# A list schedule with new TensorE estimates: cost by form and tiling, changes of tiling counted, matmuls of the present tiling taken first

## The chip, the cores and the metric

The kernel runs on one core of one Trainium2 chip, in one launch. The metric is the time on the device in microseconds (us). The engines have short names in the rows: PE is TensorE, DVE is VectorE, ACT is ScalarE, POOL is GpSimd, SP is SyncE, which issues the DMAs.

## The reference, cut to what matters

Two blocks of two layers each, over 512 tokens of width 1024, all in float32:

```python
for layer in range(2):                       # first block
    x = x + 0.5 * swiglu(rms_norm(x, g), w_gate, w_up, w_down)
    h, mem_n = rms_norm(x, g2), rms_norm(mem, g3)
    mix = mlstm_mixer(h, mem_n, ...) if layer == 0 else dilated_mixer(h, mem_n, k_sh, v_sh, ...)
    x = x + mix
    x = x + 0.5 * swiglu(rms_norm(x, g4), ...)
    if layer == 0: k_sh, v_sh = ...          # shared keys and values, from x
for l in range(2):                           # second block, on x and a context of 256 tokens
    shift, scale, gate = split(silu(c) @ w_mod[l] + b_mod[l])         # and the same from c_ctx
    u = (x * (1 + scale) + shift) @ w_in[l]
    y = concat(rwkv7_both_directions(u), grouped_attention(u), neighbourhood_attention(u)) * silu(gates)
    x = layer_norm(alpha * x + gate * (y @ w_out[l]))
```

The recurrence of the second block (`S = S * decay - (S k) b + v k`, token by token, forward and backward) is what the kernel does in chunks of 32 tokens.

## The kernel before, in words

The kernel is written as if for a NeuronCore, but its calls are only recorded: each becomes an `Op` (line 354) on named tiles, with an estimated time (`_cost`, line 364). `schedule` (line 529) then fixes the order of issue for all engines at once and gives every tile a numbered slot of its kind (`SLOTS`, line 265: 8 PSUM banks `ps`, 4 slots `raw` for weights as loaded, 70 tiles `t` and so on). `emit` (line 552) issues the operations in that order; so every instruction in the profile has the line 568.

`simulate` (line 441) is the list schedule. It is run from the end, which gives each operation a due time (its key), and from the front, where each engine takes, of the operations that are ready, the one with the least key; three such rounds are made. For TensorE there is one exception: operations are either "small" (estimated under 0.1 us, line 362) or not, and one of the present kind is preferred as long as its key is at most `STAY` = 2.0 us behind the best one's (lines 271, 488, 493). `LATENCY` (line 267) is the time from the end of an operation to the start of one that depends on it.

The large products (`proj`, line 698, and `ffn`, line 803) are split in two parts per operand, so three fp32r matmuls of 128x128 weights and up to 512 columns stand for one in float32. All others are float32 matmuls, each of which shows as two records in the trace. Many of them use a part of the array, as their operands have fewer than 128 partitions or fewer than 128 columns of weights. In this text a tiling is such a part, rows by columns, as the rows write it (128\*32: 128 rows, 32 columns). Those that the prediction speaks of:

- 128\*32, `modulation` (line 1358): each of four quarters of the columns of w_mod goes to its own 32 columns of the array (line 1369), 32x512 or 32x256 outputs; `sums` (line 729) does the same with blocks of tokens.
- 128\*64: the outputs of the attentions (`attend`, line 1531), and in the recurrence `pz` (line 1814) and the state's update; two positions, columns 0 and 64.
- 64\*64 and 64\*32: reads of the state S in the chain over the chunks (`rwkv_d`, line 1822).
- In `rwkv_c` (line 1792) the two matmuls of a step have different tilings: `pu` (line 1813, 128\*128) and `pz` (line 1814, 128\*64).

Of the kernel before, what the change touches and what calls it, by code (L numbers as in the profile page):

```python
# [16 lines left out]
P = 128  # L17
# [6 lines left out]
# ------------------------------------------------------------------ host layouts  # L24
# [5 lines left out]
def _wt(w, ksplit=1):  # L30
    """[K, M] -> [M/128, ksplit, 128, K/128/ksplit*128]: one contiguous block per load."""
    k, m = w.shape
    a = w.reshape(ksplit, k // P // ksplit, P, m // P, P).transpose(3, 0, 2, 1, 4)
    return a.reshape(m // P, ksplit, P, -1)


def _wk(w):
    """[K, N] -> [128, K/128*N]: k tiles side by side."""
    k, n = w.shape
    return w.reshape(k // P, P, n).transpose(1, 0, 2).reshape(P, -1)  # L40
# [71 lines left out]
def _rot():  # L112
    """The lhsT of the rope rotation [-x2, x1, -x4, x3] in each half of 64."""
    m = np.zeros((P, P), np.float32)
    for o in (0, 32, 64, 96):
        for j in range(16):
            m[o + 16 + j, o + j] = -1.0
            m[o + j, o + 16 + j] = 1.0
    return m
# [11 lines left out]
def _order(strict):  # L131
    """[128 = (half, beta or eta, i), direction, head parity, chunk of pair, t]: i up to t in the direction's order, in
    the half that holds the chunk; strict: i before t, and eta alone."""
# [28 lines left out]
def _masks():  # L162
    """Selectors of the first block, loaded where they are used."""
# [7 lines left out]
def pack(a):  # L171
    """Lays the inputs out for the chip: permutations, paddings and copies only."""
# [25 lines left out]
    # second block: tiles r3 k3 v3 dd|ad, rg3, aq3, ak, ag3, nq2, nk2, ng2; token-major av|nv  # L198
    q6 = np.arange(384).reshape(6, 64)[[0, 3, 1, 4, 2, 5]].reshape(-1)
    for l in range(2):  # L200
# [9 lines left out]
        # [3 blocks, 8 k tiles, 128, 1024]  # L210
# [22 lines left out]
def _dil_bias(rel):  # L233
    """[4 heads, 128 queries, 512]: previous and own block of group 0, group 1, group 2; entries of rel_bias or NEG."""
# [11 lines left out]
# neighbourhood attention: tokens in the order (column, row); a tile of 128 queries (16 columns) sees 256 keys from here  # L246
# [3 lines left out]
def _na_bias(rpb):  # L250
    """[2 pairs of heads, 4 tiles, 128 queries, 2 x 256 keys]: entries of rpb, or NEG outside the window of columns."""
# [10 lines left out]
# ------------------------------------------------------------------ recording, order and on-chip memory  # L262
# The program is recorded first, as operations on named tiles. A list schedule over estimated times then fixes the
# order in which the operations are issued, and for every tile one of the numbered slots of its kind.
SLOTS = dict(t=70, raw=4, ps=8, big=3, uv=1, S=14, tmp=2, s8=48, s32=16, s64=4)
ENGINES = ("tensor", "vector", "scalar", "gpsimd", "sync")
LATENCY = dict(tensor=0.2, vector=0.14, scalar=0.15, gpsimd=0.15, sync=3.0)
# [24 lines left out]
class Ref:  # L292
    """A recorded tile, or a view of it. v: numbers of the cells it covers, a cell being a column of 32 partitions."""
# [43 lines left out]
class Recorder:  # L337
    """Stands for the NeuronCore: notes (engine, method, arguments) in the current list."""
# [15 lines left out]
class Op:  # L354
    def __init__(self, eng, method, a, k):
# [4 lines left out]
        self.reads = [x for w, x in refs if not w]  # L360
        self.cost = self._cost()
        self.small = self.cost < 0.1 and eng == "tensor"

    def _cost(self):
        """Estimated microseconds on the engine."""
        n = max([x.cols() for x in self.writes + self.reads] or [1])
        ps = any(x.base.kind == "ps" for x in self.reads)
        if self.eng == "tensor":
            n = self.writes[0].cols()
            if self.method == "transpose":  # L370
                return 0.84e-3 * n
            l = self.k["lhsT"]
            f = 1 / 2.4 if l.base.dt == F32R else 4 / 2.4
            half = 0.58 if 16 < l.cols() <= 64 else 1.0
            return 0.002 + 1e-3 * max(n, 64) * f * half
# [15 lines left out]
def weave(parts):  # L391
    """One order for independent lists of operations, each spread evenly by cost."""
# [9 lines left out]
def dependences(ops):  # L402
    """For each operation the earlier ones that it has to follow."""
    writer, readers, last_pe = {}, {}, {}     # per tile: the last writer of each cell; reads since: (operation, cells)
# [36 lines left out]
def simulate(ops, before, after, key, lag, ahead):  # L441
    """A list schedule: of the operations that are ready and whose tiles have slots, each engine takes the one of least
    key. Only the one of least key overall may take the last slots. lag(i, j): time from the end of i to the start of j."""
# [6 lines left out]
    empty = {k: [(0.0, i) for i in range(m)] for k, m in SLOTS.items()}     # (time, slot) of free slots  # L450
    ready, free = [0.0] * n, dict.fromkeys(ENGINES, 0.0)
    wait = {e: [] for e in ENGINES}       # (time, operation): inputs complete at a later time
    can = {e: [] for e in ENGINES}        # (key, operation)
    small = False
# [5 lines left out]
    def room(i, tight):  # L460
        """When the slots that operation i needs are free; None if there are none."""
# [11 lines left out]
    def best(tight):  # L473
        out = None
        for e in ENGINES:
# [4 lines left out]
            for src, time in ((can[e], lambda x: free[e]), (wait[e], lambda x: x[0])):  # L480
                pick = None
                for x in sorted(src):
# [5 lines left out]
                    if pick and ops[i].small != small:  # L488
                        continue
                    at = room(i, tight)  # L490
                    if at is not None:
                        pick = (max(at, time(x)), key[i], i, e, src, x)
                        if e != "tensor" or src is not can[e] or ops[i].small == small:
# [7 lines left out]
    while len(order) < n:  # L501
# [6 lines left out]
        if e == "tensor":  # L508
            small = ops[i].small
# [19 lines left out]
def schedule(ops):  # L529
    """The order of issue, and a slot per tile: a schedule made from the end gives the latest start of each operation;  # L530
    one from the front takes the operations by that. Each further round makes the schedule from the end by the last one
    from the front."""
# [8 lines left out]
    lag = lambda i, j: 0.0 if ops[i].eng == ops[j].eng == "tensor" else LATENCY[ops[i].eng]  # L541
# [10 lines left out]
def emit(tc, ops):  # L552
    """Issues the recorded operations through Tile."""
# [17 lines left out]
# ------------------------------------------------------------------ the program  # L571
class Prog:
# [13 lines left out]
    # ---- memory  # L586
# [9 lines left out]
    def t2(self, shape=(P, T), dt=F32):  # L596
        """A tile of up to 2 KB a partition; two small ones from the same place in the program share a slot."""
# [28 lines left out]
    # ---- order  # L626
    def par(self, *parts):
        """Independent parts of the program, woven together."""
# [9 lines left out]
    # ---- small helpers  # L638
# [29 lines left out]
    def tr(self, out, a):  # L668
        """PE transpose of 128 partitions, exact."""
        self.nc.tensor.transpose(out, a, self.idn)  # L670

    def split(self, h, l, src, scale=None):
        """src (times a per-partition scale) as the exact sum of two 12-bit parts."""
# [7 lines left out]
    def loadw(self, src, n, w):  # L681
        """n columns of weights as parts, a pair per w columns."""
# [15 lines left out]
    def proj(self, src, xh, xl, n=T, cut=None):  # L698
        """One feature-major tile: out[m, t] = sum_d w[d, m] x[d, t]; cut: ranges of tokens, one after the other."""
# [7 lines left out]
    def proj_tm(self, src, ncol, xh, xl, sels):  # L707
        """Token-major: out[t, n] = sum_d x[d, t] w[d, n]; src [128, 8*ncol], k tiles side by side."""
# [8 lines left out]
    def pow(self, out, a):  # L717
        """out = a ** -0.5."""
# [4 lines left out]
    def rsqrt(self, out, src, n, scale, eps):  # L723
        """out = (src * scale + eps) ** -0.5 for n columns."""
# [4 lines left out]
    def sums(self, tiles, nt):  # L729
        """PSUM [128 = i, t, 2 j + h] = sum over half h of the partitions of tiles[j][:, (t, i)]; the tokens' blocks are  # L730
        summed side by side on the tensor engine."""
# [7 lines left out]
    def turn(self, ps, nt):  # L739
        """PSUM [32 nt, 128] transposed, [128, nt, 32]."""  # L740
# [6 lines left out]
    def parts(self, n=T, cnt=KD):  # L747
        """cnt pairs of [128, n] tiles for the parts of a split."""
# [7 lines left out]
    def norm(self, src, gain, n=T):  # L756
        """The parts of gain*x, and the sum over feature tiles of x**2 / 1024."""
# [1320 lines left out]
```

## Time and profile before

| what | value |
|---|---|
| time, median of 3 runs | 3384.07 us (3383.62 to 3389.64) |
| profiled execution, span | 3384.7 us |
| TensorE busy | 3282.6 us, 97% of the span, 21302 matmul records |
| VectorE, ScalarE, GpSimd busy | 65%, 48%, 7% of the span |
| mean granted TensorE clock | 0.987 of full speed |

The profiled execution's only time is its span, from the first instruction to the last; it stands 0.6 us above the median of the runs. In a timeline row, the start of one row less the start of the one before is the time that the earlier row took of the engine; the second number of a row is longer, since it runs to the end of the last matmul, which the next ones overlap. A float32 matmul counts as x2 there, an fp32r matmul as x1.

### The profile page before, as it was taken

What the parts mean: (1) busy time and instruction counts of PE and PEld (TensorE: products, weight loads), DVE (VectorE), ACT (ScalarE), POOL (GpSimd) and SP (SyncE); (2) the same over time, 40 slices, a digit from 0 to 9 for tenths busy, and PEclk for the clock granted to TensorE, in tenths of its full rate; (3) what the DMA queues carried; (4) which work ended last, traced back from release to release, by engine and by line L of the source; (5) the groups of instructions that cost most, each with busy time, mean ns of one, the idle gap of its engine ahead of it and who ended that gap; (6) DMA issues with size and microseconds to landing.
All of it is one profiled execution on the core that took longest, in us unless ns stands there. A gap on an engine that the chain in (4) does not pass through costs nothing.

```text
span 3384.7 us, 55344 instructions
## 1 busy us (share of the span) xinstructions
PE 3282.6 (97%) x21302; PEld 2604.3 (77%) x21302; DVE 2188.4 (65%) x4605; ACT 1611.1 (48%) x3577; POOL 241.4 (7%) x233
## 2 busy tenths in 40 slices
PE   8999999999999999999999999999999898999898
PEld 4688878878877788767887788777777677877677
DVE  5455578475578676444567846677575787585876
ACT  3333455363434345322345735343553873654773
POOL 0000000000000101000001000000121011010101
PEclk9999999999999999999999999999999999999999
DMA  6434433123222333444332332223322233322231
GB/s 212 152 122 130 138 102 107 53 81 108 93 68 88 110 127 117 138 137 132 95 105 74 116 95 89 72 89 107 111 72 81 73 113 101 109 85 87 60 119 47
DMA packets 153489, 348.41 MB, mean 103 GB/s; under 512 B 16645, under 2 KB 60421, under 8 KB 153225
## 3 DMA queue, kind: packets, MB, share of 16 engines
q1 hardware_dynamic: 153224, 344.87, 32.0%
q8 instruction: 167, 2.74, 0.3%
q14 instruction: 98, 0.79, 0.1%
HBM read 315.05 MB, written 29.76 MB: 102 GB/s over the span
## 4 chain that ended last, share of the span: by engine, by line
PE 84%; DVE 7%; ACT 5%; issue 1%; DMA 1%; POOL 1%; SPq 0%; ACTq 0%; POOLq 0%; DVEq 0%
PE ps L568 84%; DVE t L568 5%; ACT t L568 4%; ACT big L568 1%; DVE big L568 1%; DVE s L568 1%; DVE tmp L568 1%; POOL s L568 1%; DMA raw<-in_wgu_dram 1%; ACT uv L568 0%; DMA raw<-in_aw_dram 0%; DMA raw<-in_win_dram 0%; DMA raw<-in_wmod_dram 0%; DVE uv L568 0%; SPq L568 0%
## 5 line engine op out<-in xcount | busy, mean ns | idle before, releaser
L568 PE MATMUL ps<-t,t 128*128 128x512 f32 (+6 forms) x15204 | 2880.3, 352 | 48.2 <-ACT t L568 26.3
L568 PEld LDWEIGHTS ps<-t,t 128*128 128x128 f32 (+2 forms) x15204 | 2282.3, 182 | 549.9 <-issue 93.1
L568 ACT ACTIVATE t<-raw 128x512 fp32r<-128x512 f32 (+1 forms) x962 | 565.0, 612 | 777.3 <-PE ps L568 526.1
L568 DVE TENSOR_TENSOR t<-raw,t 128x512 fp32r<-128x512 f32 (+2 forms) x962 | 626.2, 671 | 295.8 <-PE ps L568 197.4
L568 ACT ACTIVATE t<-t 128x512 f32<-128x512 f32 (+8 forms) x739 | 376.8, 525 | 448.1 <-DVE t L568 251.6
L568 DVE TENSOR_TENSOR t<-t,t 128x256 f32<-128x256 f32 (+7 forms) x812 | 417.8, 544 | 110.7 <-ACT t L568 62.5
L568 DVE TENSOR_TENSOR t<-ps,t 128x512 f32<-128x512 f32 (+3 forms) x274 | 178.9, 658 | 236.7 <-PE ps L568 229.3
L568 ACT ACTIVATE t<-ps 128x512 f32<-128x512 f32 (+9 forms) x446 | 215.0, 513 | 233.2 <-PE ps L568 230.6
L568 POOL TENSOR_TENSOR s<-s,const 128x4 f32<-128x4 f32 (+6 forms) x65 | 99.3, 1530 | 1788.9 <-DVE s L568 1780.6
L568 DVE SCALAR_TENSOR_TENSOR t<-ps,t 128x512 f32<-128x512 f32 (+3 forms) x229 | 148.1, 649 | 106.1 <-PE ps L568 105.2
L568 PE MATMUL ps<-const,t 128*128 128x128 f32 (+1 forms) x1116 | 188.0, 289 | 20.3 <-ACT t L568 11.8
L568 PEld LDWEIGHTS ps<-const,t 128*128 128x128 f32 x1116 | 134.7, 147 | 64.8 <-ACT t L568 27.9
L568 PE MATMUL ps<-uv,t 64*64 64x64 f32 (+1 forms) x2208 | 143.9, 229 | 3.4 <-DVE t L568 1.6
L568 PEld LDWEIGHTS ps<-uv,t 64*64 64x64 f32 (+1 forms) x2208 | 103.3, 135 | 53.0 <-issue 14.4
L568 ACT ACTIVATE t<-t,const 128x256 f32<-128x256 f32 (+3 forms) x165 | 102.0, 645 | 68.8 <-DVE t L568 37.2
L568 ACT ACTIVATE uv<-ps 32x128 f32<-32x128 f32 (+1 forms) x288 | 92.2, 321 | 59.4 <-PE ps L568 55.3
L568 DVE SCALAR_TENSOR_TENSOR t<-t,t 128x512 f32<-128x512 f32 (+2 forms) x116 | 76.6, 662 | 57.6 <-ACT t L568 56.3
L568 DVE TENSOR_TENSOR uv<-uv,ps 32x192 f32<-32x192 f32 x192 | 66.6, 347 | 66.3 <-PE ps L568 58.7
L568 POOL TENSOR_TENSOR S<-S,s 128x192 f32<-128x192 f32 x96 | 62.4, 650 | 601.0 <-DVE S L568 451.7
L568 PE MATMUL ps<-S,t 64*32 64x64 f32 x2112 | 104.1, 224 | 1.0 <-DVE S L568 1.0
L568 ACT ACTIVATE t<-ps,s,s 128x256 f32<-128x256 f32 (+1 forms) x140 | 88.2, 652 | 32.8 <-DVE s L568 32.7
L568 ACT ACTIVATE t<-ps,const 128x256 f32<-128x256 f32 (+1 forms) x100 | 57.1, 576 | 75.6 <-PE ps L568 74.9
(81 smaller groups left out, 1390.4 us busy)
## 6 DMA issues: line engine op xcount, KB each, us to landing
raw<-in_wgu_dram SPq DMA_DIRECT2D x176, 512.0 KB, 3.8
raw<-in_win_dram SPq DMA_DIRECT2D x88, 512.0 KB, 3.7
raw<-in_wd_dram SPq DMA_DIRECT2D x128, 256.0 KB, 2.7
raw<-in_wmod_dram SPq DMA_DIRECT2D x48, 512.0 KB, 3.8
t<-dram SPq DMA_DIRECT2D x68, 256.0 KB, 3.0
dram<-t SPq DMA_DIRECT2D x68, 256.0 KB, 2.0
t<-dram SPq DMA_DIRECT2D x97, 128.0 KB, 2.3
raw<-in_wd_dram SPq DMA_DIRECT2D x64, 192.0 KB, 2.4
```

Source lines behind the costliest of these rows:

```text
L568: getattr(getattr(tc.nc, op.eng), op.method)(*map(real, op.a), **{q: real(v) for q, v in op.k.items()})
```

## The change

The planner's numbers for TensorE are new, and its preference for "the present kind" now goes by the tiling and no longer by the size. Every comment and docstring is also gone, which moves the line of issue from 568 to 583. No operation is added or taken away: both kernels issue the same 17224 matmuls, 4607 VectorE, 3303 ScalarE and 238 GpSimd instructions and 1043 on SyncE's queue; their order and the slots of their tiles differ.

```diff
-LATENCY = dict(tensor=0.2, vector=0.14, scalar=0.15, gpsimd=0.15, sync=3.0)
+LATENCY = dict(tensor=0.22, vector=0.13, scalar=0.15, gpsimd=0.15, sync=3.0)
+INTO_PE = 0.12
+
+SIDE_BY_SIDE = {(128, 128): 1, (128, 64): 2, (128, 32): 4, (64, 128): 2, (64, 64): 4, (64, 32): 6, (32, 128): 4,
+                (32, 64): 6, (32, 32): 8}
+RETILE = 0.12
...
-        self.small = self.cost < 0.1 and eng == "tensor"
+
+    def _tiling(self):
+
+        l = self.reads[0] if self.method == "transpose" else self.k["lhsT"]
+        up = lambda n: 32 if n <= 32 else 64 if n <= 64 else 128
+        return up(32 * l.v.shape[0]), up(l.cols())
...
             if self.method == "transpose":
-                return 0.84e-3 * n
-            l = self.k["lhsT"]
-            f = 1 / 2.4 if l.base.dt == F32R else 4 / 2.4
-            half = 0.58 if 16 < l.cols() <= 64 else 1.0
-            return 0.002 + 1e-3 * max(n, 64) * f * half
+                return 0.003 + 0.833e-3 * n
+            if self.k["lhsT"].base.dt == F32R:
+                return 0.0137 + n / 2400
+            one = max(0.003 + n / 1200, 0.11 if self.tiling[1] == P else 0.08)
+            return 2 * max(one / SIDE_BY_SIDE[self.tiling], 0.02)
...
-                    if pick and ops[i].small != small:
+                    same = ops[i].tiling == tiling
+                    if pick and not same:
                         continue
...
-                        if e != "tensor" or src is not can[e] or ops[i].small == small:
+                        if e != "tensor" or src is not can[e] or same:
                             break
...
-        if e == "tensor":
-            small = ops[i].small
+        if e == "tensor" and ops[i].tiling != tiling:
+            at, tiling = at + RETILE, ops[i].tiling
...
-    lag = lambda i, j: 0.0 if ops[i].eng == ops[j].eng == "tensor" else LATENCY[ops[i].eng]
+    def lag(i, j):
+        pe = ops[j].eng == "tensor"
+        return 0.0 if pe and ops[i].eng == "tensor" else LATENCY[ops[i].eng] + INTO_PE * pe
+
```

What it does to the order of TensorE is shown at three places. In these rows ps, t, raw, uv and const are tiles with their running numbers, which differ between the kernels, and the last word is the size of the output; a row with x4 is four equal instructions.

The first is the start of the program: raw is w_mod of the modulation, and the 128x512 rows are the first product of the feed-forward. Before:

```order
L568 MATMUL ps_185<-raw_149,const_92 32x512
L568 MATMUL ps_183<-t_133,t_178 128x512
L568 MATMUL ps_185<-raw_149,const_92 32x512
L568 MATMUL ps_183<-t_139,t_170 128x512
L568 MATMUL ps_183<-t_133,t_170 128x512
L568 MATMUL ps_183<-t_141,t_178 128x512
L568 MATMUL ps_183<-t_145,t_170 128x512
L568 MATMUL ps_185<-raw_161,const_92 32x512 x2
L568 MATMUL ps_183<-t_141,t_170 128x512
```

After the change:

```order
L583 MATMUL ps_179<-raw_143,const_92 32x512 x2
L583 MATMUL ps_179<-raw_170,const_92 32x512 x2
L583 MATMUL ps_199<-t_133,t_193 128x512
L583 MATMUL ps_199<-t_139,t_187 128x512
L583 MATMUL ps_199<-t_133,t_187 128x512
L583 MATMUL ps_199<-t_145,t_193 128x512
L583 MATMUL ps_199<-t_150,t_187 128x512
```

The modulation's matmuls come two at a time, and the first four are ahead of the feed-forward.

The second is some 200 rows further: the modulation's last block of columns (raw, 32x256 outputs), again beside the feed-forward. Before:

```order
L568 MATMUL ps_709<-raw_643,const_92 32x256
L568 MATMUL ps_696<-t_444,t_646 128x512
L568 MATMUL ps_696<-t_538,t_652 128x512
L568 MATMUL ps_696<-t_543,t_646 128x512
L568 MATMUL ps_709<-raw_643,const_92 32x256
L568 MATMUL ps_696<-t_538,t_646 128x512
L568 MATMUL ps_696<-t_617,t_652 128x512
L568 MATMUL ps_696<-t_623,t_646 128x512
L568 MATMUL ps_709<-raw_643,const_92 32x256
L568 MATMUL ps_696<-t_617,t_646 128x512
L568 MATMUL ps_709<-raw_643,const_92 32x256
```

After the change:

```order
L583 MATMUL ps_179<-raw_590,const_92 32x512 x2
L583 MATMUL ps_684<-raw_616,const_92 32x256 x4
L583 MATMUL ps_672<-t_443,t_605 128x512
L583 MATMUL ps_672<-t_436,t_605 128x512
L583 MATMUL ps_697<-const_230,t_688 128x128 x4
```

The four quarters of one w_mod tile stood apart, one to three other matmuls between them, and now follow each other.

The third is in the recurrence's `rwkv_c` of the second layer: the 64x128 rows are `pz` (128\*64), the 128x64 rows `pu` (128\*128). Before:

```order
L568 MATMUL ps_29557<-t_27846,t_29478 128x512
L568 MATMUL ps_29587<-t_29573,t_29141 64x128
L568 MATMUL ps_29589<-t_29575,t_29573 128x64 x2
L568 MATMUL ps_29587<-t_29573,t_29141 64x128
L568 MATMUL ps_29589<-t_29575,t_29573 128x64
L568 MATMUL ps_29587<-t_29573,t_29141 64x128
L568 MATMUL ps_29589<-t_29575,t_29573 128x64
L568 MATMUL ps_29587<-t_29573,t_29141 64x128
L568 MATMUL ps_29557<-t_27864,t_29591 128x512
```

After the change:

```order
L583 MATMUL ps_29600<-uv_27791,t_29122 64x64 x2
L583 MATMUL ps_29603<-t_29591,t_28917 64x128 x4
L583 MATMUL ps_29608<-t_29594,t_29591 128x64 x4
L583 MATMUL ps_29573<-t_27840,t_29610 128x512
L583 MATMUL ps_29573<-t_27891,t_29373 128x512
```

The two kinds took turns, one by one, and now come four and four.

Over the whole order of TensorE, the number of times that an instruction has another tiling than the one before it goes from 1523 to 1246. The table counts stretches (instructions of one tiling in succession) and rounds (as many of them as have positions of their own in the array, so that a second instruction at a position begins a new round):

| tiling, output columns | stretches before, after | rounds before, after |
|---|---|---|
| 128\*128, all | 560, 447 | not counted |
| 128\*32, 512 | 44, 18 | 44, 21 |
| 128\*32, 256 | 41, 13 | 42, 18 |
| 128\*32, 128 | 37, 33 | 46, 48 |
| 128\*64, 128 | 180, 119 | 445, 428 |
| 128\*64, 64 and 193 | 209, 191 | 409, 401 |
| 64\*128 and 32\*128 | 52, 42 | 80, 76 |
| 64\*64 | 136, 128 | 494, 493 |
| 64\*32 | 265, 256 | 472, 464 |

## Rows read from the trace of the kernel before

**Rows 1.** The page: the span and section 1, busy us of each engine.

```profile
span 3384.7 us, 55344 instructions
...
PE 3282.6 (97%) x21302; PEld 2604.3 (77%) x21302; DVE 2188.4 (65%) x4605; ACT 1611.1 (48%) x3577; POOL 241.4 (7%) x233
```

**Rows 2.** The page's section 4, the chain that ended last, by engine.

```profile
PE 84%; DVE 7%; ACT 5%; issue 1%; DMA 1%; POOL 1%; SPq 0%; ACTq 0%; POOLq 0%; DVEq 0%
```

**Rows 3.** Windows: stretch, length, busy us of engines, granted clock, DMA share, GB/s.

```profile
0.00:250.00 250.00, 238.98 (x1057) 166.46 (x1058) 123.68 (x224) 91.64 (x173) 7.74 (x12) 1.00 0.49 163
...
2650.00:2900.00 250.00, 227.14 (x2385) 190.43 (x2384) 199.64 (x507) 167.75 (x411) 29.71 (x31) 0.95 0.31 96
...
3150.00:3385.00 235.00, 206.24 (x2239) 167.35 (x2237) 175.10 (x454) 139.17 (x347) 23.37 (x26) 0.94 0.24 76
```

**Rows 4.** Waits of PE: for whom, us in total, times, the longest.

```profile
PE ps L568 <- ACT t L568: 40.4, 46, 4.0
...
PE ps L568 <- DMA raw<-in_wmod_dram: 11.0, 1, 11.0
...
PE ps L568 <- DVE uv L568: 1.5, 4, 0.5
PE ps L568 <- DVE S L568: 1.0, 2, 0.7
```

**Rows 5.** Timeline of PE near 1565 us: start, length, tiling, form, records.

```profile
1565.44 0.64 PE L568 MATMUL ps<-raw,const 128*32 128x256 f32 x8
1566.01 1.20 PE L568 MATMUL ps<-t,t 128*128 128x512 f32 x4
1567.13 0.62 PE L568 MATMUL ps<-raw,const 128*32 128x256 f32 x2
1567.68 0.73 PE L568 MATMUL ps<-t,t 128*128 128x512 f32 x2
1568.35 0.62 PE L568 MATMUL ps<-raw,const 128*32 128x256 f32 x2
1568.90 1.88 PE L568 MATMUL ps<-t,t 128*128 128x512 f32 x7
1570.71 0.62 PE L568 MATMUL ps<-raw,const 128*32 128x256 f32 x2
```

**Rows 6.** Timeline of PE, 31 to 39 us.

```profile
31.17 1.07 PE L568 MATMUL ps<-raw,const 128*32 128x512 f32 x8
32.17 5.75 PE L568 MATMUL ps<-t,t 128*128 128x512 f32 x24
37.85 1.04 PE L568 MATMUL ps<-raw,const 128*32 128x512 f32 x2
38.82 0.73 PE L568 MATMUL ps<-t,t 128*128 128x512 f32 x2
```

**Rows 7.** Timeline of PE, 2719 to 2721 us.

```profile
2718.92 1.09 PE L568 MATMUL ps<-t,t 128*64 128x128 f32 x14
2719.93 0.66 PE L568 MATMUL ps<-const,t 128*128 128x128 f32 x4
2720.52 0.43 PE L568 MATMUL ps<-t,t 128*64 128x128 f32 x2
2720.89 0.66 PE L568 MATMUL ps<-const,t 128*128 128x128 f32 x4
```

**Rows 8.** Groups by form, PE: records, busy us and mean ns, idle before.

```profile
L568 PE MATMUL ps<-t,t 128*64 128x128 f32 x1448 | 142.0, 286 | 2.3 <-ACT t L568 1.4 <-ACT uv L568 0.3 <-DVE t L568 0.2
...
L568 PE MATMUL ps<-raw,const 128*32 128x512 f32 x128 | 48.9, 619 | 11.0 <-DMA raw<-in_wmod_dram 11.0
L568 PE MATMUL ps<-t,t 128*128 128x64 f32 x288 | 44.8, 276 | 0.4 <-ACT uv L568 0.3
...
L568 PE MATMUL ps<-raw,const 128*32 128x256 f32 x128 | 25.5, 391 | 0.0
```

**Rows 9.** A window at the start, columns as in Rows 3.

```profile
10.00:15.00 5.00, 3.98 (x5) 0.65 (x5) 4.24 (x8) 3.77 (x8) 0.00 (x0) 1.00 1.04 400
```

More of the change, by code (lines that the diff above doesn't have):

```diff
@@ L360, in __init__ @@
         self.reads = [x for w, x in refs if not w]
+        self.tiling = self._tiling() if eng == "tensor" else None
         self.cost = self._cost()
-        self.small = self.cost < 0.1 and eng == "tensor"
+    def _tiling(self):
+        l = self.reads[0] if self.method == "transpose" else self.k["lhsT"]
+        up = lambda n: 32 if n <= 32 else 64 if n <= 64 else 128
+        return up(32 * l.v.shape[0]), up(l.cols())
     def _cost(self):
@@ L453, in simulate @@
     can = {e: [] for e in ENGINES}
-    small = False
+    tiling = None
     first, head, done, order = sorted(range(n), key=key.__getitem__), 0, [False] * n, []
```

## The prediction

> **What bounds the kernel now.** I read the page's section 1 first: TensorE is busy for 3282.6 of 3384.7 us [rows 1], so all its idle time together is 102.1 us. The chain that ended last says the same from the other side: 84% of it is TensorE's own work, VectorE and ScalarE together have 12% [rows 2]. Then the windows: in the first 250 us TensorE works 239.0 us, and nearly all of what is missing is the first load (11.0 us, one wait [rows 4]); only near the end does it wait much, 22.9 us from 2650 to 2900 and 28.8 us from 3150 to 3385 [rows 3]. So a change that only reorders has two places to act: the 102 us of waiting, and whatever part of the 3283 us of "busy" is not work but the way from one matmul to the next. The second is read from the timeline, where the start of a row less the start of the row before is what that row cost.
>
> **What a change of tiling costs, and what a matmul alone in its tiling costs.** Around 1565 us TensorE alternates between 128\*128 products and the modulation's 128\*32 matmuls [rows 5]. Seven fp32r matmuls take 1570.71 - 1568.90 = 1.81 us, two take 1568.35 - 1567.68 = 0.67; so one more costs 0.228 us, and each such stretch has 0.21 us on top for being entered and left. A 128\*32 stretch costs 0.55 us with one matmul of 256 columns (1567.13 to 1567.68) and 0.57 with four (1565.44 to 1566.01): the four quarters of the array run side by side, and one alone wastes the other three. With 512 columns one takes 0.97 us (37.85 to 38.82) and four 1.00 (31.17 to 32.17) [rows 6]. From 0.55 and 0.97 a round of 512 columns is some 0.84 us, one of 256 some 0.42, and the fixed part of a stretch 0.13. For 128\*64 one matmul of 128 columns takes 0.37 us (2720.52 to 2720.89) and seven, in four rounds of two positions, 1.01 (2718.92 to 2719.93) [rows 7]: 0.213 us a round and 0.157 fixed.
>
> **The sum.** No instruction is added or removed, so every term is a count from the order (the table of stretches and rounds) times one of these prices.
>
> - 128\*128 stretches: 560 to 447. At 0.21 us the 113 are worth 23.7. The price is read from fp32r matmuls; 80 of the 113 begin with one, which gives 16.8. I take 20.
> - 128\*32: with 512 columns 26 stretches at 0.13 and 23 rounds at 0.84, 22.7 us; with 256 columns 28 at 0.13 and 24 at 0.42, 13.7 us; with 128 columns nothing (4 stretches fewer, 2 rounds more). Together 36. That is over half of these forms' busy time, 48.9 and 25.5 us [rows 8], and the second place of the order shows why it can be: one w_mod tile made four stretches of one and now makes one of four.
> - 128\*64: with 128 columns 61 stretches at 0.157 and 17 rounds at 0.213, 13.2 us; the other widths 18 at 0.157 and 8 rounds at about half, 3.7 us. Together 17. Part of it is `rwkv_c`, the third place, whose `pu` matmuls show the same thing: 144 of them (288 records) are busy 44.8 us [rows 8], 0.31 us each, while they alternate with `pz`.
> - The other tilings lose 27 stretches; at 0.157 that is 4 us, an estimate, as no row here prices them.
>
> Sum 77 us of 3282.6. All of it is TensorE's own time and so on the path, except where something else ends last.
>
> Two things come back. At the start the third TensorE instruction now waits for the second w_mod tile, and the feed-forward's first product is queued behind it; on SyncE's queue that tile stands two DMAs of 0.5 MB behind the first. At the 400 GB/s that the window from 10 to 15 us shows [rows 9], 1 MB is 2.6 us; before, work began at 11.0 us with the first tile. Between 0 and 4 us; I take 2. And in the last quarter of TensorE's order, where it waits for ScalarE and VectorE anyway, about 70 of the 277 changes go (809 to 741), a quarter of the sum, 19 us. There a shorter TensorE waits longer for the same chain; I let 8 of the 19 go back, between 0 (all of it lies in the filled parts) and 19.
>
> The new latencies and costs (fp32r 512 columns 0.227 us where the old estimate was 0.215; the row says 0.228) also move ready times on all engines. What that does to the 102 us of waiting the trace of before cannot show. Bounds: waits on ScalarE's and VectorE's tiles may fall by half of the 40.4 us that the largest group has [rows 4], or grow by as much as the present waits near the end, some 25 us in a window [rows 3]. I take nothing.
>
> 3384.7 - 77 + 2 + 8 = 3317.7 us on the profiled execution's span. That execution is 0.6 us above the median of the runs, so 3317 for the median.
>
> A page speaks for a smaller price. The Trainium skill, "TensorEngine Tiling (Array Packing)", section Key Properties, says that a change of tiling mode, not of the tile alone, drains TensorE; "TensorE: Matmul & The Clock Gate", section Step-by-step, puts a drain at about 128 cycles, which at 2.4 GHz would be 53 ns by estimate. Then 277 changes would be worth 15 us. The rows show more per change: 0.21 us for the two ends of an fp32r stretch and 0.13 to 0.16 for those of a narrow one, so a way there and back costs some 0.35 us, not 0.11; and the matmul that runs alone is not in that rule at all.
>
> **The rivals.**
>
> - *The planner's better times also shorten the waits.* For: half of the waiting is on ScalarE's and VectorE's tiles [rows 4], which the added 0.12 us into TensorE would let the planner see coming. Against: TensorE's new speed gives the others less time. 32 us less waiting gives 3285.
> - *Part of the gain becomes waiting.* A stretch of four is issued only when all four have their inputs; raw has four slots, and a w_mod tile that waits for its partner keeps a slot from the weights. For: ScalarE and VectorE are busy 67% and 80% from 2650 to 2900 [rows 3]. Against: in the first 250 us, where most of the modulation's gain lies, TensorE waits only for the first load, and DMA is half idle (0.49). Half of the 77 us gone: 3346.
> - *Only the changes count, not the rounds.* If four quarters in succession still ran one after the other here, because each waits for its load, 277 changes at 0.15 us are 42, less the 10 that come back: 3353. Against: the 0.57 us for four [rows 5].
> - *A change costs what a drain costs*, 53 ns, and nothing else: 3370. The rows speak against it, as shown.
> - *Slower: the preference holds back the recurrence.* A matmul of the chain over the chunks may now stand behind up to 2.0 us of work of the present tiling; before, all large matmuls were one kind. The chain enters TensorE twice a chunk, 16 chunks in two layers and 8 in two contexts, 96 times: at most 192 us. It decides from 77 us, 40% of that, and at half it gives 3317 + 96 = 3413. For: the waits of the last 735 us. Against: TensorE waits only 1.5 and 1.0 us for the chain's own tiles uv and S [rows 4], so the chain has slack, and keys still come first beyond 2 us.
>
> **How the numbers follow.** Forecast 50% (its own range 3298 to 3335: the sum between 65 and 85, the returns between 0 and 20). Shorter waits 14%, half returned 20%, changes alone 7%, drain alone 3%, slower 6%. What a measurement of this kernel can tell from no change is 0.2%, 6.8 us. All cases but the last are beyond that on the fast side, with a little of each lost to "same": faster 0.91, same 0.04, slower 0.05. The range 3282 to 3352 takes in the shorter waits and most of the half returned; left out are changes alone, drain, slower and the tails, under 2 in 10.
>
> **What would show it.** If the sum is right, TensorE's busy time falls to about 3210 us and the idle time stays near 110; the modulation's groups fall from 48.9 and 25.5 us to about 25 and 12, the 128\*64 group of 128 columns from 142.0 to about 130, the 128\*128 group of 64 columns from 44.8 to under 36; the stages before 2450 us shorten by some 55 us, those after by little. If the drain rule holds, the modulation's groups stay. If the recurrence is held back, waits on uv and S grow from 2.5 us to tens, in the last third. It would be wrong in kind if TensorE's busy time fell as said and the span did not.

## The result and the profile after

The changed kernel takes 3326.6 us (median of 4 runs, 3323.7 to 3333.6); the kernel before, beside it, 3385.3 us (3383.6 to 3389.6). The ratio is 0.9826, with a 95% interval of 0.9812 to 0.9840. The forecast was 3317, its range 3282 to 3352.

The page of the changed kernel: the span, section 1 (busy us of each engine) and section 4 (the chain that ended last).

```profile
span 3324.6 us, 55306 instructions
...
PE 3211.6 (97%) x21302; PEld 2597.8 (78%) x21302; DVE 2196.5 (66%) x4605; ACT 1612.8 (49%) x3577; POOL 259.9 (8%) x233
...
PE 79%; DVE 10%; ACT 5%; issue 3%; DMA 1%; POOL 1%; SPq 0%; ACTq 0%; POOLq 0%; DVEq 0%
```

Against [rows 1] TensorE is busy 71.0 us less, and idle 113.0 us instead of 102.1; so the span is 60.1 us shorter. The other engines' busy time is the same within some 20 us. In [rows 2] TensorE's own part of the chain was 84%, now 79%.

Where along the program it went is read from windows (length, busy us of the engines, granted clock). The kernel before, and then the changed one, each up to about its 13,000th matmul record and from there to the end:

```profile
0.00:2450.00 2450.00, 2414.38 (x12984) 1908.58 (x12985) 1525.39 (x3036) 1068.06 (x2301) 121.49 (x113) 1.00 0.34 109
2450.00:3384.70 934.70, 868.21 (x8319) 695.71 (x8318) 662.98 (x1569) 543.06 (x1277) 119.94 (x120) 0.96 0.27 86
```

```profile
0.00:2390.00 2390.00, 2353.09 (x12996) 1906.73 (x12997) 1524.45 (x3039) 1070.45 (x2306) 137.28 (x113) 0.99 0.34 112
2390.00:3324.60 934.60, 858.46 (x8307) 691.09 (x8305) 672.02 (x1566) 542.37 (x1272) 122.66 (x120) 0.96 0.27 86
```

The same number of records is done 60 us sooner, so the whole gain lies in the first part, which has all of the modulation. None remains from the last part, in which seven tenths of the recurrence's matmuls on uv and S run: there TensorE is busy 9.7 us less and idle as much longer. (The order differs, so it is the same number of records and not record for record the same ones.)

The groups by form of the changed kernel (records, busy us, mean ns of one, idle before), for those of [rows 8] and three others:

```profile
L583 PE MATMUL ps<-t,t 128*128 128x512 f32 x9120 | 2260.5, 396 | 11.6 <-DVE t L583 8.4 <-ACT t L583 2.8
...
L583 PE MATMUL ps<-t,t 128*64 128x128 f32 x1448 | 128.0, 285 | 1.9 <-DVE t L583 0.9 <-ACT uv L583 0.6 <-ACT t L583 0.2
L583 PE MATMUL ps<-S,t 64*32 64x64 f32 x2112 | 103.3, 227 | 1.8 <-DVE S L583 1.6
...
L583 PE MATMUL ps<-uv,t 128*64 128x64 f32 x1056 | 92.0, 238 | 6.3 <-DVE t L583 3.4 <-DVE uv L583 1.8 <-ACT t L583 1.0
...
L583 PE MATMUL ps<-t,t 128*128 128x64 f32 x288 | 40.4, 272 | 1.6 <-ACT uv L583 1.3 <-DVE t L583 0.2
...
L583 PE MATMUL ps<-raw,const 128*32 128x512 f32 x128 | 26.3, 632 | 10.7 <-DVE t L583 10.1 <-DMA raw<-in_wmod_dram 0.5
...
L583 PE MATMUL ps<-raw,const 128*32 128x256 f32 x128 | 10.2, 389 | 0.0
```

The modulation's two groups fall by 22.6 and 15.3 us. The mean of one record is unchanged (632 and 389 ns, were 619 and 391): each matmul takes as long as before, but four of them now share that time. The timeline shows it where [rows 5] had rows of x2 (start, length, tiling, form, records):

```profile
1451.51 0.64 PE L583 MATMUL ps<-raw,const 128*32 128x256 f32 x8
1452.08 7.78 PE L583 MATMUL ps<-t,t 128*128 128x512 f32 x33
```

The stretch is a foursome (x8 records) and costs 0.57 us, as the one foursome of [rows 5] did.

### The profile page after: what moved, and what is told of

The parts are those of the page before. It is cut to its first block, busy times and chain, and to the rows that moved or that the text cites. A ratio compares the mean times of both kernels' runs of the same rounds, so it can differ in the third digit from the quotient of the medians.

```text
span 3324.6 us, 55306 instructions
## 1 busy us (share of the span) xinstructions
PE 3211.6 (97%) x21302; PEld 2597.8 (78%) x21302; DVE 2196.5 (66%) x4605; ACT 1612.8 (49%) x3577; POOL 259.9 (8%) x233
## 4 chain that ended last, share of the span: by engine, by line
PE 79%; DVE 10%; ACT 5%; issue 3%; DMA 1%; POOL 1%; SPq 0%; ACTq 0%; POOLq 0%; DVEq 0%
PE ps L583 79%; DVE t L583 7%; ACT t L583 3%; DVE big L583 1%; POOL s L583 1%; DVE s L583 1%; DVE tmp L583 1%; ACT uv L583 1%; ACT big L583 1%; DMA raw<-in_wgu_dram 1%; DVE uv L583 0%; DMA raw<-in_wd_dram 0%; DMA raw<-in_wmod_dram 0%; DMA raw<-in_wkv_dram 0%; DMA dram<-t 0%
## 5 line engine op out<-in xcount | busy, mean ns | idle before, releaser
L583 PE MATMUL ps<-t,t 128*128 128x512 f32 (+6 forms) x15204 | 2839.3, 351 | 44.6 <-DVE t L583 23.4
L583 POOL TENSOR_TENSOR s<-s,const 128x2 f32<-128x2 f32 (+6 forms) x65 | 111.0, 1709 | 1762.8 <-DVE s L583 1762.7
L583 PE MATMUL ps<-const,t 128*128 128x128 f32 x1116 | 188.7, 291 | 30.8 <-DVE t L583 17.4
L583 ACT ACTIVATE t<-t,const 128x256 f32<-128x256 f32 (+3 forms) x165 | 101.9, 646 | 45.0 <-DVE t L583 25.8
L583 ACT ACTIVATE t<-ps,s,s 128x256 f32<-128x256 f32 (+1 forms) x140 | 87.8, 641 | 30.3 <-DVE s L583 25.9
L583 PEld LDWEIGHTS ps<-S,t 64*32 64x32 f32 x2112 | 61.1, 107 | 43.4 <-issue 15.4
```

The costliest lines, as they stand in the source:

```text
L583: getattr(getattr(tc.nc, op.eng), op.method)(*map(real, op.a), **{q: real(v) for q, v in op.k.items()})
```

## The experiments

The theory: TensorE's order by tiling is the whole gain, and its size is the number of stretches and rounds saved times the prices of the prediction. The rivals: the better numbers (costs, latencies) bring it; only the number of changes counts; the price is that of a drain. A question came with the first results: what does the granted clock take back?

For that, the span of each profiled run is split in three. *Idle* is the span less TensorE's busy time. *Clock* is what the stretches at half clock cost: in a run the granted clock is 1.00 or 0.50 of full speed, and an alternation of two small forms that took 0.49 us at full clock took 0.76 at half (shown below), so I count 1 - 0.49/0.76 = 0.355 of the time that TensorE is busy at 0.50. This is an estimate, and a low one, since wider matmuls lose more (below). *Work* is the rest, TensorE's time as if at full clock. *Priced* is the change in work that the counts of the order and the prediction's prices give (0.18 us, 20/113, for a 128\*128 stretch). Each ratio is to runs of the kernel before that were taken beside it (medians 3385.3 to 3387.8 us). The split is of one profiled execution, while the executions of one kernel lie up to 20 us apart, so a few us in it decide nothing.

| kernel | time | ratio to before, 95% | idle | clock | work, change | priced |
|---|---|---|---|---|---|---|
| before | 3385.3 | 1 | 102.1 | 20.4 | 0 | 0 |
| after | 3326.6 | 0.9812 to 0.9840 | 113.0 | 29.0 | -79.6 | -78.4 |
| e1_tiling_only | 3323.4 | 0.9803 to 0.9832 | 101.9 | 31.0 | -74.5 | -78.9 |
| e2_numbers_only | 3422.6 | 1.0088 to 1.0138 | 109.3 | 48.6 | -3.4 | -11.9 |
| e9_latencies_only | 3427.3 | 1.0099 to 1.0129 | 108.5 | 37.6 | +13.8 | +11.9 |
| e10_costs_only | 3407.0 | 1.0043 to 1.0073 | 98.0 | 46.7 | +2.3 | -0.9 |
| e3_all_but_narrow | 3340.9 | 0.9852 to 0.9885 | 106.7 | 25.6 | -59.6 | -59.5 |
| e8_stay1 | 3360.7 | 0.9901 to 0.9946 | 118.6 | 39.8 | -57.9 | -54.5 |
| e5_stay4 | 3327.1 | 0.9805 to 0.9835 | 118.6 | 42.7 | -97.7 | -99.9 |
| e6_no_retile | 3333.2 | 0.9829 to 0.9858 | 118.4 | 42.3 | -87.8 | -93.7 |
| e12_reads_first | 3298.0 | 0.9720 to 0.9751 | 122.1 | 28.8 | -123.7 | -114.7 |
| e14_reads_e1 | 3289.7 | 0.9701 to 0.9733 | 107.6 | 24.2 | -111.7 | -106.2 |
| e16_reads_e1_stay3 | 3300.8 | 0.9719 to 0.9765 | 123.8 | 38.7 | -122.4 | -118.1 |
| e18_reads_e1_f32r | 3289.4 | 0.9692 to 0.9724 | 109.8 | 28.4 | -108.9 | -109.5 |

Over all these orders, the work follows the priced counts within 9 us. How much of that hangs on the 0.355 is seen from fp32r matmuls of 512 columns in a stretch at half clock of the changed kernel (the second row is the matmul behind the six):

```profile
905.55 2.77 PE L583 MATMUL ps<-t,t 128*128 128x512 f32 x6
908.11 0.63 PE L583 MATMUL ps<-t,t 128*128 128x512 f32 x1
```

Each takes 0.427 us where [rows 5] has 0.228, a loss of 0.47. With 0.47 throughout, the changed kernel's work is -82.4 and its clock 11.4 us more than before (8.6 in the table), and work and priced counts lie up to 12 us apart.

**The preference alone, and the numbers alone.** The first is the kernel before with nothing new but the kind that is preferred:

```diff
-        self.small = self.cost < 0.1 and eng == "tensor"
+        self.small = self._tiling() if eng == "tensor" else None
```

> The kernel before, with one edit: the preference goes by the tiling and no longer by the size; all estimated times and latencies stay old. In TensorE's order the stretches of 128*128 fall from 560 to 440, the modulation's 512-column ones from 44 to 24 (rounds 44 to 25), the 256-column ones from 41 to 17 (42 to 20), changes of tiling from 1523 to 1244. Theory (the order by tiling is the gain): TensorE's busy time falls by some 72 us to about 3211, as in the changed kernel, idle time 100 to 125, time about 3328 (3315 to 3345). Rival (the new costs and latencies are the gain): within 10 us of the kernel before, 3375 to 3385.

The second has all the new numbers and the old kinds, and no cost for a change of tiling:

```diff
-                    same = ops[i].tiling == tiling
+                    same = ops[i].small == small
...
-        if e == "tensor" and ops[i].tiling != tiling:
-            at, tiling = at + RETILE, ops[i].tiling
+        if e == "tensor":
+            small = ops[i].small
```

> The changed kernel's costs and latencies, with the old preference by size and no price for a change of tiling. Stretches of 128*128 561 (before 560), modulation 512 columns 34 (44), 256 columns 34 (41), changes 1502 (1523): by the prices of the prediction 12 us less of TensorE. Theory (the order by tiling is the gain): busy time about 3271, time about 3374 (3360 to 3390). Rival (the numbers are the gain, above all by shorter waits): idle time well under 100 us, time 3330 or less.

The preference alone gives 3323.4 us; its interval and that of the whole change overlap. The numbers alone are slower than before by 0.9 to 1.4%, at neither the 3374 of the theory nor the 3330 of the rival. So the gain is the order by tiling, and the numbers, beside it, are worth nothing that can be measured. Where the numbers alone lose is read from the page of that kernel and its windows:

```profile
span 3416.6 us, 55323 instructions
...
PE 3307.4 (97%) x21302; PEld 2633.8 (77%) x21302; DVE 2190.1 (64%) x4605; ACT 1611.7 (47%) x3577; POOL 263.4 (8%) x233
```

```profile
3254.00:3274.60 20.60, 17.18 (x153) 13.57 (x151) 13.65 (x29) 13.91 (x39) 0.00 (x0) 1.00 0.38 112
3274.60:3301.90 27.30, 26.90 (x216) 18.77 (x212) 10.33 (x27) 13.62 (x37) 2.41 (x4) 0.50 0.07 21
3301.90:3325.00 23.10, 23.10 (x307) 17.82 (x306) 15.80 (x48) 13.36 (x42) 2.54 (x5) 1.00 0.39 109
```

Of 166.0 us at half clock (before: 85.4) 27.3 are one stretch. Behind 3.4 us of waiting in 20.6 the clock falls, TensorE then does 216 records in 27.3 us, and when the clock is back 307 in 23.1. Of the 31.9 us that this run is longer, 28.2 are the clock, 7.2 more idle time, and -3.4 work.

**The two kinds of numbers apart**, on the old preference: new latencies only (`LATENCY`, `INTO_PE` and `lag` of the diff), and new costs only (the kernel above with the old `LATENCY` and `INTO_PE` 0).

> The kernel before with the new latencies alone (0.22 and 0.13 instead of 0.2 and 0.14, and 0.12 into TensorE); old costs, old preference. By the prices 12 us more of TensorE's work (128*128 stretches 587 instead of 560, changes 1591 instead of 1523). If the latencies are what made the numbers alone slow (more waiting and more time at the lower clock): 3410 or above, with over 140 us at the lower clock. If they are harmless: 3387 + 12, about 3399, lower clock as before, some 85 to 105 us.

> The new costs alone: old latencies, old preference, no price for a change. By the prices 1 us less than before (574 stretches, 1569 changes, 33 and 34 modulation stretches). If the costs are what made the numbers alone slow: 3410 or above, with over 140 us at the lower clock. If they are harmless: about 3386. If neither of the two is slow, the slowness of both together is an accident of one order.

Both are slower than before, 1.1% and 0.6%. With the latencies the work itself grows by 13.8 us, close to the 11.9 that the counts give: the order has more stretches; the clock takes 17.2 us more. With the costs the work is nearly unchanged (+2.3) and the clock takes 26.3 us more. Both have over 140 us at the lower clock (144.2 and 162.4). Neither shortens the waits by anything like the 32 us of the first rival (idle +6.4 and -4.1 us).

**All but the modulation's tiling.** 128\*32 counts as 128\*128, both for the preference and for the cost of a change:

```diff
+        self.kind = (P, P) if self.tiling == (P, 32) else self.tiling
...
-                    same = ops[i].tiling == tiling
+                    same = ops[i].kind == tiling
```

> The changed kernel, but for the preference and the price of a change the 128*32 tiling counts as 128*128, so these matmuls are again taken as they come. Changes of tiling stay low, 1260 (changed kernel 1246), but the modulation has 34 stretches and 34 rounds of 512 columns (changed kernel 18 and 21) and 34 and 35 of 256 (13 and 18). Theory (a round that runs alone wastes the other positions): 19 us of TensorE more than the changed kernel, the two modulation groups at about 38 and 21 us busy (26.3 and 10.2 in the changed kernel), time about 3344. Rival (only the number of changes of tiling counts): 14 changes at 0.15 us, so no more than 3 us above the changed kernel, 3329.

The order has 1260 changes of tiling, the whole change 1246; yet 3340.9 us against 3326.6, with intervals that do not touch. The modulation's groups of this kernel and a piece of its timeline:

```profile
L585 PE MATMUL ps<-raw,const 128*32 128x512 f32 x128 | 40.6, 633 | 11.3 <-DMA raw<-in_wmod_dram 11.3
...
L585 PE MATMUL ps<-raw,const 128*32 128x256 f32 x128 | 21.8, 391 | 0.0
```

```profile
1471.09 0.96 PE L585 MATMUL ps<-t,t 128*128 128x512 f32 x3
1471.98 0.62 PE L585 MATMUL ps<-raw,const 128*32 128x256 f32 x2
1472.53 0.50 PE L585 MATMUL ps<-t,t 128*128 128x512 f32 x1
```

They keep 14.3 and 11.6 us that the whole change takes out; over all groups the work is 20.0 us more, 19 were expected. A single matmul here has its stretch of 0.55 us to itself again. The number of changes alone is not the measure; how many matmuls run side by side within one stretch counts too. The Trainium skill's rule from "TensorEngine Tiling (Array Packing)", Key Properties, that a change of mode drains TensorE, has no term for this; the row, 0.55 us for one and 0.57 for four, decides.

**How long the preference may hold out**, and without the cost of a change: `STAY` 1.0 and 4.0 instead of 2.0, `RETILE` 0.0 instead of 0.12.

> The changed kernel with STAY 1.0 instead of 2.0. Changes 1333 (1246), 128*128 stretches 486 (447), modulation rounds 28 and 20 (21 and 18): 24 us more of TensorE's work by the prices. Theory: about 3349 at the same waits and clock. Rival (a smaller preference holds back less, so that less waiting pays for it): 3330 or less.

> The changed kernel with STAY 4.0 instead of 2.0: a matmul of the present tiling is preferred up to 4 us behind the best one. Stretches of 128*128 385 (changed kernel 447), changes 1123 (1246), modulation rounds 23 and 18 (21 and 18), 128*64 stretches of 128 columns 99 (119). Theory (stretches are what counts, waits stay): 22 us by the prices, some 19 by the ratio that the change itself showed (71 of 78), so busy about 3192, time about 3308. Rival (the preference holds back the chains that other engines wait for): busy falls as said, idle time grows from 113 us by as much or more, time 3326 or above.

> The changed kernel without the planner's price for a change of tiling (RETILE 0 instead of 0.12 us). The order has even fewer changes, 1181 (1246); 128*128 stretches 411 (447); 15 us less by the prices. Theory (stretches are what counts): about 3312. Rival (the price in the plan keeps the plan's times true, and without it waits and the lower clock grow): 3327 or above. In either case the span should be that of TensorE's work by the prices at full clock, plus its idle time, plus half of its busy time in the stretches where the lower clock is granted, to within 8 us.

At 1.0 the kernel takes 3360.7 us, 34 more than at 2.0; in the profiled runs, 38.1 us apart, 21.7 are work that comes back, 10.8 clock and 5.6 waiting. At 4.0 TensorE's work falls by another 18.1 us, and 13.7 of clock and 5.6 of idle time take that back: 3327.1, no difference. Without `RETILE` it is the same: 8.2 us less work, 13.3 more for the clock, 5.4 more idle, and 3333.2 where I had expected a gain. So these orders with fewer stretches have less work (18.1 of 21.5 us priced, and 8.2 of 15.3) and aren't shorter. The rival of `STAY` 4.0 named 3326 or above, which is right, but by idle time alone; most of it is the clock. The sum that was expected to hold without `RETILE`, with half of the time at half clock counted as lost, gives 3338 us for the span of 3335.1, within its 8 us.

**The best use of it.** In the state's read-out (`rwkv_d`) the code itself records, for each half `a`, four 64\*32 reads and two 128\*64 products in turn, and both add into the same `ps` tiles, which ties their order. The loops changed places:

```diff
-            for a in range(2):
-                for j in range(3):
+            for j in range(3):
+                for a in range(2):
                     for i, par in ((0, 0), (0, 1), (1, 0), (1, 1)):
...
+                for a in range(2):
                     for par in range(2):
```

This was done in the changed kernel (e12_reads_first) and in the one with the preference alone (e14_reads_e1); the latter again with `STAY` 3.0 and with the old cost of fp32r matmuls raised by 6%, `f = 1.06 / 2.4`.

> The changed kernel with one loop of the recurrence's outputs written in another order: for each j the eight reads of the old states (64*32) come first and then the four products with u and v (128*64), where before four and two took turns. Same matmuls, same sums. Changes of tiling 1057 (changed kernel 1246), 64*32 stretches 177 (256), 128*64 stretches of 64 columns 104 (186), 128*128 stretches 422 (447). Theory (stretches and rounds at the prices of the rows): 36 us less of TensorE's work than the changed kernel, time about 3292 (3280 to 3305). Rival (what is left bounds it elsewhere, the chain over the chunks through VectorE): idle time takes it back, 3315 or above.

> The same loop order in the kernel that has the preference by tiling and all old numbers. Changes 1110 (1244 without the loop), 28 us less by the prices. Theory: 3323 - 27, about 3296. If the new numbers matter only for how well the rest is filled, this one and the same with the new numbers are within 10 us of each other.

> The fastest kernel so far (preference by tiling, old numbers, reads of the states first) with STAY 3.0. Changes 1040 (1110), 12 us less of TensorE's work by the prices. With waits and clock as there: about 3278. If a larger preference costs waits and clock, as it did in the changed kernel with 4.0: 3290 or above.

> The same fastest kernel with one number changed: the estimate of an fp32r matmul of 512 columns 0.228 instead of 0.215 us, which is what the rows show. Changes 1080 (1110), 3 us less by the prices. About 3287 if waits and clock stay; what it differs from that, by the lower clock and the waits, is the scatter that any small change of the plan brings.

The timeline of the changed kernel at full clock, in the read-out, and of e12_reads_first:

```profile
3040.41 0.30 PE L583 MATMUL ps<-S,t 64*32 64x64 f32 x2
3040.64 0.33 PE L583 MATMUL ps<-uv,t 128*64 128x64 f32 x2
3040.90 0.30 PE L583 MATMUL ps<-S,t 64*32 64x64 f32 x4
3041.13 0.33 PE L583 MATMUL ps<-uv,t 128*64 128x64 f32 x2
3041.39 0.53 PE L583 MATMUL ps<-S,t 64*32 64x64 f32 x12
```

```profile
2729.71 0.66 PE L583 MATMUL ps<-S,t 64*32 64x64 f32 x28
2730.30 0.46 PE L583 MATMUL ps<-uv,t 128*64 128x64 f32 x8
2730.69 0.34 PE L583 MATMUL ps<-S,t 64*32 64x64 f32 x16
2730.96 0.46 PE L583 MATMUL ps<-uv,t 128*64 128x64 f32 x8
```

One or two 64\*32 matmuls cost 0.23 us and one 128\*64 matmul 0.26 in the first; in the second eight 64\*32 in succession cost 0.27 and four 128\*64 0.39. The two groups fall accordingly; of e12_reads_first, to be laid beside those of the changed kernel above:

```profile
L583 PE MATMUL ps<-S,t 64*32 64x64 f32 x2112 | 78.4, 224 | 1.0 <-DVE S L583 0.5 <-ACT t L583 0.4
...
L583 PE MATMUL ps<-uv,t 128*64 128x64 f32 x1056 | 64.6, 234 | 1.4 <-DVE uv L583 0.8 <-DVE t L583 0.6
```

24.9 and 27.4 us less. Some 8 of these 52 us are in other groups again: TensorE's whole busy time falls by 44.3 us (36 were expected), 9.1 come back as waiting, and the profiled run is 35.2 us shorter than the changed kernel's. By the medians it is 28.6, to 3298.0 us. On the preference alone it gives 3289.7, which is 2.7 to 3.0% faster than before and beats both kernels; the cost raised by 6% changes nothing (3289.4), and `STAY` 3.0 loses more than it saves: 10.7 us less work, 14.5 more for the clock, 16.2 more idle in the profiled runs (3300.8, the longer time expected).

## Why the prediction was right, and where it was not

The span fell by 60.1 us where 67 were forecast: work -79.6 where -77 was said, idle +10.9 where +10, and +8.6 us of clock where nothing was said. By place, the first part is 60.0 us shorter where the sum gives 56 (77, less the 19 of the last part and the 2 of the start); the last part was to be 11 us shorter and is not.

- *128\*32, 36 us.* Right: the two groups fell by 37.9, and e3_all_but_narrow puts 25.9 us back into them by undoing this part alone. Two readings beside it were off: 36 of 74.4 us is just under half, not over it, and not most of the gain but half, 18.9 us, lies in the first 250 us.
- *128\*128 stretches, 20 us.* The fp32r group with 512 columns fell by 22.7 us from this row of the kernel before:

```profile
L568 PE MATMUL ps<-t,t 128*128 128x512 f32 x9120 | 2283.2, 398 | 11.3 <-ACT t L568 9.8 <-DVE t L568 1.0 <-ACT big L568 0.2
```

Of this group 19.7 us stood at half clock before and 13.8 after, by its records in these stretches, which is some 2.7 of the 22.7 (at 0.47). So 20 us are left, as was taken; the group holds other effects too.
- *128\*64.* For 128 columns 13.2 was said, 14.0 measured. For 64 and 193 columns 3.7 was said. The group with 193 columns fell from 6.1 to 4.0 us; the `uv` group did not fall, it went up to 92.0 from this row:

```profile
L568 PE MATMUL ps<-uv,t 128*64 128x64 f32 x1056 | 89.9, 233 | 2.8 <-DVE t L568 1.6 <-DVE uv L568 1.1
```

The clock explains the rise and no more: 6.1 us of this group stand at half clock in the changed kernel, next to nothing before. At 0.355 these are 2.2 us, so at full clock the group would stand near 89.8, as before. That is an estimate.
- *`pu`, from 44.8 to under 36.* Wrong in size: 40.4. The third place of the order, four and four, was taken for all of them. Counted over the whole order, the 144 `pu` stand in 75 runs before and in 55 after, 39 and 16 of them right behind a `pz`. 20 runs at 0.21 us are 4.2, and 4.4 were measured, which fits the price, though no run tests it for `pu` alone. The count had been read from one place. The term for 128\*128 stretches, on which the sum rests, was counted over the whole order and is not touched.
- *The other tilings, 4 us.* Their groups (64 rows and fewer) go from 230.1 to 229.4 us. In them the time at half clock rose from 4.8 to 18.1 us, which would hide 4.7 at 0.355; this too is an estimate.
- *The start, 2 us.* Not as a wait:

```profile
10.14 1.92 PE L583 MATMUL ps<-raw,const 128*32 128x512 f32 x4 [10.14 <-DVE t L583]
12.58 1.92 PE L583 MATMUL ps<-raw,const 128*32 128x512 f32 x4 [0.52 <-DMA raw<-in_wmod_dram]
14.44 2.80 PE L583 MATMUL ps<-t,t 128*128 128x512 f32 x11
```

The feed-forward's first product starts at 14.44 us; before, it started 1.6 us sooner, on this row of its timeline:

```profile
12.84 0.80 PE L568 MATMUL ps<-t,t 128*128 128x512 f32 x1
```

But what stands ahead of it is work, four of the modulation's matmuls where there was one. The third TensorE instruction waits 0.52 us for its tile and the first starts 0.9 us sooner (10.14 for 11.02), so up to this product TensorE is idle 10.7 us where it was idle 11.0: none of the 2 us came as waiting.

- *The waits.* TensorE's waits (for whom, us, times, the longest): one row of the kernel before that [rows 4] leaves out, and those of the changed kernel:

```profile
PE ps L568 <- DVE t L568: 23.6, 19, 6.9
...
PE ps L583 <- DVE t L583: 56.9, 33, 10.1
PE ps L583 <- ACT t L583: 28.8, 32, 4.9
PE ps L583 <- DVE uv L583: 3.7, 6, 1.1
...
PE ps L583 <- DVE S L583: 1.6, 4, 0.5
```

ScalarE's largest group is shorter by 11.6 us and VectorE's longer by 33.3, 10.1 of which is the start (the first load, which had that wait before). The recurrence was not held back: uv and S together 5.3 us, were 2.5, no tens. What returned lies in VectorE's tiles. That the waits do not shrink with the new numbers, e9 and e10 show.

That +10.9 stands so near to +10 is luck as far as the runs show. The reason given was that a shorter TensorE waits longer for the same chain. But e1_tiling_only, with nearly the same work taken out, is idle 101.9 us, no longer than before. Its last part, for the rows above:

```profile
2394.40:3320.60 926.20, 860.33 (x8319) 694.18 (x8317) 669.44 (x1569) 545.80 (x1277) 115.97 (x120) 0.95 0.27 87
```

That is 65.9 us idle; before it was 66.5, and with the whole change 76.1. In three pairs that differ in the new numbers (after and e1, e12 and e14, e2 and before) the side with them is idle 7 to 15 us longer, where the prediction took nothing for them. By these orders the two terms were off by about as much, in opposite directions. Against that stand e10_costs_only, idle 4.1 us less than before, and e14_reads_e1, which has the old numbers and 111.7 us less work and is idle 5.5 us longer. With one profiled run an order, and idle times that scatter by 26 us, the cause of the 10.9 stays open.
- *The clock*, the step that was missing. Before, 57.4 us of busy time stood at half clock, now 81.6. Windows of the changed kernel, with one of the two longest such stretches in which TensorE works in the middle, and its alternations in the timeline:

```profile
2690.00:2707.60 17.60, 15.92 (x194) 11.71 (x194) 9.87 (x24) 13.48 (x33) 1.53 (x3) 1.00 0.40 121
2707.60:2721.30 13.70, 13.70 (x128) 9.96 (x128) 6.78 (x19) 5.55 (x19) 1.01 (x2) 0.50 0.07 21
2721.30:2740.00 18.70, 18.62 (x280) 14.15 (x282) 14.97 (x42) 10.71 (x30) 3.88 (x6) 1.00 0.58 192
```

```profile
2712.88 0.47 PE L583 MATMUL ps<-uv,t 128*64 128x64 f32 x2
2713.29 0.43 PE L583 MATMUL ps<-S,t 64*32 64x64 f32 x4
2713.64 0.47 PE L583 MATMUL ps<-uv,t 128*64 128x64 f32 x2
```

A pair takes 0.41 + 0.35 = 0.76 us here and 0.23 + 0.26 = 0.49 at full clock. Across the fourteen orders the clock costs between 20.4 and 48.6 us by this share, a spread as wide as that of their idle time (98.0 to 123.8). What in an order makes it fall stays open: it fell behind waits, as in e2_numbers_only, and stayed low while TensorE was busy all the time, in 13.70 us of 13.70 above. No run here changed that alone.

Of the rivals, the drain alone (3370) and the changes alone (3353) fall with the groups, and the latter with e3_all_but_narrow; the shorter waits (3285) with e9 and e10 and with the idle time of the change itself; the recurrence held back (3413) with the waits. Half of the gain turned into waiting (3346) did not happen: of the 79.6 us of work 10.9 went back as idle time. With `STAY` 4.0 and without `RETILE` it comes nearer to that, 38.8 us of 97.7 and 38.2 of 87.8, but more of it in clock (22.3 and 21.9) than in waiting.

## What to carry to other kernels

Where TensorE is busy nearly all the time with matmuls on parts of the array, count over the whole order how many stretches of one tiling it has and how many positions each stretch fills, and price both from the timeline: here that gave the work of thirteen changed orders within 9 us (12, with the other share for the clock), while the new estimates in the planner gave nothing that could be measured. Matmuls of one tiling belong together, in the planner's preference and in the order in which code adds into one accumulator; holding out longer for them (`STAY` 4.0 and 3.0 for 2.0) no longer paid here. Before a fall in work is booked as time, look at the granted clock and the idle time of the new order: between them they took back what the last refinements saved.

## What the runs showed of the hardware

- Four float32 matmuls at the four positions of 128\*32 cost what one costs, 0.57 us against 0.55 with 256 columns.
- The granted clock stood at 0.50, 1.2 GHz, for 13.70 us in which TensorE was busy throughout, with 128 records of small matmuls and of 128\*128 among them; 18.7 us with 280 records behind it ran at 1.00.
- At that clock an alternation of two small forms took 1.55 times as long (0.76 us for 0.49), an fp32r matmul of 512 columns 1.87 times (0.427 us for 0.228).
